# Which up-projection units sum their weights on VectorE: three in the first layer, one in the second

## The chip, the core and the metric

The kernel runs on one core of a Trainium2 chip. Its time is the device time of one launch in microseconds; three runs gave 2179.67, 2180.15 and 2181.21 us (median 2180.15). One more execution was taken with the hardware profiler: it took 2179.59 us, and its span from the first to the last instruction is 2177.8 us. TensorE multiplies, VectorE (DVE) and ScalarE (ACT) do the elementwise work, GpSimd (POOL) and SyncE (SP) issue transfers; POOL also computes a few small powers.

## The reference

Two layers of an encoder on 256 positions of width 2048, all in float32. The part that the change touches is the gated MLP that ends each layer:

```python
D_MODEL, SEQ, D_FF = 2048, 256, 5632

def conv_ffn(x, w_up, conv_w, conv_b, w_down):
    u = x @ w_up                                   # 256 x 11264: gate | value
    up = jnp.pad(u, ((0, 0), (1, 1), (0, 0)))
    c = conv_w.astype(u.dtype)
    u = c[0] * up[:, :-2] + c[1] * up[:, 1:-1] + c[2] * up[:, 2:] + conv_b
    gate, val = jnp.split(u, 2, axis=-1)
    return (jax.nn.silu(gate) * val) @ w_down

for layer in range(2):
    h = rms_norm(x, norm_mix[layer])
    mixed = pool_and_attention(h) if layer == 0 else mlstm_mixer(h)   # shortened
    x = x + mixed
    x = x + conv_ffn(rms_norm(x, norm_ffn[layer]), w_up[layer], ...)
```

## The kernel before

Every product is made of three: an operand is split into a rounded high part and the rest, and high by high, high by low and low by high are summed in PSUM. Weights come from DRAM in chunks of 128 x 1024 (512 KB) through the class `Stream`. `load` issues a chunk's transfer on the SP queue; `split` writes the high part with a copy on ScalarE (L164) and the rest with a subtraction on VectorE (L165) into a tile `hl`. In the MLP, loads run 7 chunks ahead of TensorE and splits 3 chunks ahead, with a few buffers for each.

The order of TensorE's instructions is that of the code. The other engines' orders are made when the kernel is built, except where instructions are pinned (the weight sums on VectorE and the preparing transfers are).

**The MLP of a layer.** The 44 column tiles of the hidden width (128 gate and 128 value columns each) are done in chunks `FCH` of 4, 8, 8, 8, 8, 8 tiles. `up` makes one tile from 4 weight chunks: 64 matmuls, then a sum of two PSUM halves, a multiplication by the row scale, and `tail` (convolution, SiLU, gate, split). `down` multiplies a finished chunk of tiles by the down-projection. `_ffn_plan` lays these out as *slots*, one weight chunk each: a tile is 4 slots, a quarter of a down-projection 2 slots (first chunk) or 4 slots.

**Units.** Some halves of a chunk, four tiles, are done together by `quads` as a 2 x 2 block product with seven block products in place of eight. A unit takes 28 *steps* of 6 matmuls with 512 columns, each from one weight chunk, strewn between the slots: with `(chunk, half, lo, hi, made)` in `UNITS`, step k stands behind slot `lo + k * (hi - lo - 3) / 28` (plus 3 for the last 12 steps). The first 16 steps work through 8 pairs of chunks, the last 12 through 8 chunks with one sum each and 4 without. At its end the four tiles are transposed by `finish` (16 transposes on TensorE) and go through `tail`. A list `late` keeps a unit from starting before the one ahead of it has finished.

The weights of three of the seven products are sums of weight blocks. They are made in one of two ways, by the flag `made`:

- `made` 0: `sums` adds them on VectorE in the chunk just before it is split: per pair one addition in the first chunk (L144) and two in the second (L149, L150), and one more in each of 8 chunks of the last 12 (L147). That is 32 additions of 128 x 512 per unit.
- `made` 1: `make_step` has made them ahead of time in DRAM. Per pair of chunks four parts: twice a copy of half the rows into a DRAM tile `G` on the SP queue (L118) and an accumulating transfer from POOL's queue on top of it (L119), then two accumulating transfers within `G` (L123). The table `make` says beside which weight load each part is issued. The unit then loads `G` instead of the plain weights.

Before, both layers have four units, two of each kind, in turn. Layer 0's 16 prepared pairs are issued during the attention and during layer 0's MLP, layer 1's 16 pairs from 20 chunks before the mLSTM on, 14 chunks apart.

Activation sums for the units (`sums()`, tiles `v` and `sx`) are made once per layer on VectorE and ScalarE at the start of the MLP. `Weave` is the clock that spreads the elementwise pieces: a piece that says `yield 2.5` is issued no sooner than 2.5 us of counted TensorE work later.

Of the kernel before, what the change touches and what calls it, by code (L numbers as in the profile page):

```python
# [237 lines left out]
def trunk(ctx: ExitStack, tc: tile.TileContext, gx, xT, xn, call, catt, cml, weights, make, out):  # L238
# [37 lines left out]
    wv = Weave()  # L276
# [678 lines left out]
    def ffn_layer(layer, norm, nxt):  # L955
        with ExitStack() as es:
# [13 lines left out]
            def tail(u, f, gt, i):  # L970

                y = tp.tile([P, 2, S], F32, tag="y", name=f"y{layer}_{f}")
                for j in range(2):
                    tl = f + j * FT
                    a.activation(y[:, j, :], u[:, j, :], AF.Identity, scale=cw(tl, 1), bias=cw(tl, 3))
                    v.scalar_tensor_tensor(y[:, j, 1:S], u[:, j, 0 : S - 1], cw(tl, 0), y[:, j, 1:S],
                                           ALU.mult, ALU.add)
                    v.scalar_tensor_tensor(y[:, j, 0 : S - 1], u[:, j, 1:S], cw(tl, 2), y[:, j, 0 : S - 1],
                                           ALU.mult, ALU.add)
                s_ = y[:, 0, :]  # L980
                a.activation(s_, s_, AF.Silu)
                v.tensor_mul(s_, s_, y[:, 1, :])
                a.copy(gt[:, i, 0, :], s_)
                v.tensor_sub(gt[:, i, 1, :], s_, gt[:, i, 0, :].bitcast(F32))
# [37 lines left out]
            def product(bank, act, w, c, first, last):  # L1022

                (xh, xl), (wh, wl) = act, (w[:, j, c : c + 512] for j in range(2))
                mm(bank, xh, wh, first, False)
                mm(bank, xh, wl, False, False)
                mm(bank, xl, wh, False, last)
                wv.tick(0.68)

            def block_of(k, t):  # L1030
                return [norm.xx[:, k, j, t * P : t * P + P] for j in range(2)]

            def sum_of(j, p):
                return [sx[:, j, p, i, :] for i in range(2)]

            def quads(fs, c, i0, name):

                def bank(j):
                    return psp.tile([P, 512], F32, tag="ps", name=f"p{j}_{name}")

                def part(j):
                    return cp1.tile([P, 512], F32, tag=f"c{j}", name=f"c{j}_{name}")

                m = KT // 2
                r0, r1 = norm.rcol[:, 0:1], norm.rcol[:, 1:2]
                for p in range(m):
                    ends = p == 0, p == m - 1
                    if p == 0:
                        wv.until(lambda: not late)
                        late.update((0, 2))  # L1050
                    hl = st.next()
                    if p == 0:
                        b1, b5 = bank(1), bank(5)
                    product(b1, block_of(2 * p, 0), hl, 0, *ends)
                    product(b5, sum_of(0, p), hl, 512, *ends)
                    yield
                    hl = st.next()
                    if p == 0:
                        b6, b4 = bank(6), bank(4)
                    product(b6, sum_of(1, p), hl, 0, *ends)  # L1060
                    product(b4, block_of(2 * p + 1, 1), hl, 512, *ends)
                    if p == m - 1:
                        c12, c21, c22 = part(12), part(21), part(22)
                        a.activation(c12, b1, AF.Copy, scale=n0)
                        a.activation(c21, b1, AF.Copy, scale=r1)
                        a.activation(c22, b5, AF.Copy, scale=r1)
                        v.scalar_tensor_tensor(c12, b6, n0, c12, ALU.mult, ALU.add)
                    yield
                for p in range(m):
                    hl = st.next()  # L1070
                    product(b5, sum_of(3, p), hl, 512, False, p == m - 1)
                    product(b6, sum_of(2, p), hl, 0, False, p == m - 1)
                    if p == m - 1:
                        v.scalar_tensor_tensor(c21, b6, r1, c21, ALU.mult, ALU.add)
                        v.tensor_add(c22, c22, c21)
                        v.scalar_tensor_tensor(c21, b4, r1, c21, ALU.mult, ALU.subtract)
                        v.scalar_tensor_tensor(c12, b5, n0, c12, ALU.mult, ALU.add)
                    yield
                    if p % 2:
                        hl = st.next()  # L1080
                        for n in range(2):
                            product(b1, block_of(2 * (p - 1 + n) + 1, 0), hl, n * 512, False, p - 1 + n == m - 1)
                        if p == m - 1:
                            c11 = part(11)
                            a.activation(c11, b1, AF.Copy, scale=r0)
                            gt = g_of(c)
                            wv.add(finish(c12, c22, fs[2:], gt, i0 + 2, name), 3.0)
                            wv.add(finish(c11, c21, fs[:2], gt, i0, name), 5.0)
                        yield

            def finish(top, bottom, fs, gt, i0, name):

                for n, f in enumerate(fs):
                    tr = psp.tile([P, 2, S], F32, tag="ps", name=f"tr{layer}_{f}")
                    for j in range(2):
                        for t, src in enumerate((top, bottom)):
                            c = (2 * j + n) * P
                            pe.transpose(tr[:, j, t * P : t * P + P], src[:, c : c + P], ident)  # L1098
                    u = tp.tile([P, 2, S], F32, tag="tb", name=f"tb_{layer}_{f}")
                    a.copy(u, tr)  # L1100
                    tail(u, f, gt, i0 + n)
                    yield 2.5
                late.discard(i0 % 4)

            def down_end(gt, b, kts):
# [58 lines left out]
            def g_of(c):  # L1164
                if c not in gts:
                    gts[c] = actp.tile([P, 8, 2, S], F32R, tag=f"B{c % 2}", name=f"g{layer}_{c}")
                return gts[c]

            for step in _ffn_plan(layer):
                kind, c = step[:2]  # L1170
                key = step[:3]
                if key not in run:
                    f0 = sum(FCH[:c])
                    run[key] = (up(f0 + step[2], g_of(c), step[2]) if kind == "n" else
                                down(c, gts[c], step[2]) if kind == "d" else
                                quads([f0 + 4 * step[2] + j for j in range(4)], c, 4 * step[2], f"{layer}_{c}{step[2]}"))
                next(run[key], None)
# [64 lines left out]
def _down_chunks(w):  # L1242
# [6 lines left out]


UNITS = (
    ((2, 1, 18, 62, 0), (3, 1, 66, 94, 1), (4, 1, 98, 142, 0), (5, 1, 146, 174, 1)),
    ((2, 1, 18, 62, 0), (3, 1, 66, 94, 1), (4, 1, 98, 142, 0), (5, 1, 146, 174, 1)),
)


# [82 lines left out]
    return out  # L1339


def _make_steps(pairs, places):

    make = {}
    for (key, q), (at, gap) in zip(pairs, places):
        for part in range(4):
            make.setdefault(at + part * gap, []).append((key, part, q))
    return make


def _constants():
# [102 lines left out]
```

## Time and profile before

| | |
|---|---|
| runs, median of 3 | 2180.15 us |
| profiled execution | 2179.59 us |
| its span | 2177.8 us |
| granted TensorE clock | 1.000 |
| first MLP (first `up` to first `mv` matmul of the mLSTM) | 256.0 to 976.6 us |
| mLSTM and its output projection | 976.6 to about 1454.8 us |
| second MLP | about 1454.8 us to the end |
| units of layer 0, first step to last transposition | 310.2-478.2, 486.7-609.1, 614.7-780.0, 788.5-910.8 us |
| units of layer 1 | 1508.9-1678.7, 1687.2-1809.5, 1815.2-1980.0, 1988.5-2110.8 us |

In the rows of the profile, L285 is the line in which nearly all matmuls are recorded, so groups are told apart by their tiles: `up` for tile-wise up-projections, `p` for steps of a unit, `dn` for down-projections, `tr` for a unit's transposes. PE is the row of matmuls, PEld that of weight loads that run beside them. A group's row gives its count, its busy time with the mean of one instruction in ns, and the idle time of its engine just before it with what ended that.

### The profile page before, as it was taken

Reading aid. Unit: us, or ns where it says so; the run is one execution under the profiler, and the core shown is the slowest. Engines: PE = TensorE matmul, PEld = TensorE weight load, DVE = VectorE, ACT = ScalarE, POOL = GpSimd, SP = SyncE. Lnnn points to the kernel's source line nnn. Section 1 sums busy time; section 2 is a strip of 40 time slices with the busy share of each in tenths; the row PEclk is TensorE's granted clock in tenths of the full one; section 3 lists DMA queues with packets and bytes.
Section 4 is the critical chain, followed back from the end, with each engine's and each line's share of the span. In section 5 each row is a group of like instructions: output and inputs, shape, how many; then the busy total and the mean of one; then the engine's idle time right before and its main releaser. Section 6 shows DMA issues by size and latency. Waiting matters only on the chain.

```text
span 2177.8 us, 30504 instructions
## 1 busy us (share of the span) xinstructions
PE 2164.5 (99%) x11040; PEld 1838.1 (84%) x11040; DVE 1711.6 (79%) x2414; ACT 1277.6 (59%) x1808; POOL 133.5 (6%) x168
## 2 busy tenths in 40 slices
PE   9999999999999999999999999999999999999999
PEld 7888888888888888889888888888888888888887
DVE  7686699888798787866767676669888879979785
ACT  7665555666565575655555554556566656556663
POOL 0121101000000000001101010110000000000000
PEclk9999999999999999999999999999999999999999
DMA  8868879889978878769788777877876875767773
GB/s 324 245 217 249 236 234 295 276 264 293 301 235 287 272 232 250 262 202 253 219 248 226 238 229 219 265 223 222 269 244 223 258 247 202 258 232 233 251 232 126
DMA packets 157467, 533.18 MB, mean 245 GB/s; under 512 B 18715, under 2 KB 21059, under 8 KB 156291
## 3 DMA queue, kind: packets, MB, share of 16 engines
q1 hardware_dynamic: 139744, 493.66, 66.2%
q0 software_dynamic: 14496, 33.83, 10.5%
q10 hardware_dynamic: 3074, 3.75, 0.9%
q8 instruction: 86, 1.41, 0.3%
q14 instruction: 67, 0.54, 0.1%
HBM read 529.02 MB, written 69.25 MB: 275 GB/s over the span
## 4 chain that ended last, share of the span: by engine, by line
PE 92%; DVE 6%; issue 1%; ACT 1%; DMA 0%; ACTq 0%; SPq 0%; DVEq 0%
PE up L285 24%; PE dn L285 20%; PE p L285 13%; PE op L285 8%; PE mv L285 4%; PE mq L285 4%; PE mk L285 4%; PE mo L285 4%; PE qproj L285 3%; DVE hl L165 3%; PE pool L285 1%; PE vproj L285 1%; PE kproj L285 1%; ACT hl L164 1%; PE tr L1098 1%
## 5 line engine op out<-in xcount | busy, mean ns | idle before, releaser
L165 DVE TENSOR_TENSOR hl<-w,hl 128x1024 fp32r<-128x1024 f32 (+1 forms) x868 | 1045.0, 1216 | 334.9 <-ACT hl L164 328.1
L164 ACT CAST hl<-w 128x1024 fp32r<-128x1024 f32 (+1 forms) x867 | 897.7, 1048 | 643.7 <-PE up L285 115.8
L285 PE MATMUL up<-xx,hl 128*128 128x512 f32 (+1 forms) x3584 | 647.8, 337 | 0.0
L285 PEld LDWEIGHTS up<-xx,hl 128*128 128x128 f32 x3584 | 563.4, 188 | 87.7 <-DVE hl L165 0.4
L285 PE MATMUL dn<-hl,g 128*128 128x512 f32 x2064 | 492.7, 391 | 0.0
L285 PEld LDWEIGHTS dn<-hl,g 128*128 128x128 f32 x2064 | 385.2, 188 | 78.5
L285 PE MATMUL p<-hl,sx 128*128 128x512 f32 x768 | 206.7, 391 | 3.5 <-DVE hl L165 2.5
L285 PEld LDWEIGHTS p<-hl,sx 128*128 128x128 f32 x768 | 139.4, 188 | 30.6 <-DVE hl L165 3.8
L285 PE MATMUL p<-hl,xx 128*128 128x512 f32 x576 | 157.9, 391 | 4.6 <-DVE hl L165 4.6
L285 PEld LDWEIGHTS p<-hl,xx 128*128 128x128 f32 x576 | 104.5, 188 | 25.3 <-DVE hl L165 6.3
L119 POOL DMA_DIRECT2D G<-in_q x64 | 52.2, 816 | 984.7 <-DMA G<-in_q 972.8
L285 PE MATMUL mk<-xx,hl 128*128 128x512 f32 (+1 forms) x512 | 92.2, 338 | 0.0
L285 PE MATMUL mq<-xx,hl 128*128 128x512 f32 (+1 forms) x512 | 92.2, 338 | 0.0
L285 PE MATMUL mv<-hl,xx 128*128 128x512 f32 (+2 forms) x480 | 91.8, 351 | 0.0
L285 PE MATMUL op<-hl,cat 128*128 128x512 f32 x384 | 91.7, 394 | 0.0
L285 PE MATMUL mo<-hl,xx 128*128 128x512 f32 x384 | 90.6, 392 | 0.0
L285 PE MATMUL op<-hl,mcat 128*128 128x512 f32 x384 | 89.5, 392 | 0.0
L285 PEld LDWEIGHTS mq<-xx,hl 128*128 128x128 f32 x512 | 79.3, 188 | 11.5
L285 PEld LDWEIGHTS mk<-xx,hl 128*128 128x128 f32 x512 | 79.1, 188 | 11.3
L285 PEld LDWEIGHTS mv<-hl,xx 128*128 128x128 f32 x480 | 78.3, 189 | 11.2
L285 PEld LDWEIGHTS op<-hl,mcat 128*128 128x128 f32 x384 | 71.5, 188 | 14.6
L285 PEld LDWEIGHTS mo<-hl,xx 128*128 128x128 f32 x384 | 71.0, 188 | 14.2
(243 smaller groups left out, 1860.8 us busy)
## 6 DMA issues: line engine op xcount, KB each, us to landing
w<-in_up SPq DMA_DIRECT2D x224, 512.0 KB, 4.7
w<-in_dn SPq DMA_DIRECT2D x176, 512.0 KB, 4.6
w<-in_m_in SPq DMA_DIRECT2D x124, 512.0 KB, 5.2
w<-in_q SPq DMA_DIRECT2D x96, 512.0 KB, 4.8
G<-in_q SPq DMA_DIRECT2D x64, 512.0 KB, 5.7
w<-in_a_in SPq DMA_DIRECT2D x46, 512.0 KB, 6.1
G<-in_q POOLq DMA_DIRECT2D x64, 256.0 KB, 6.4
G<-G POOLq DMA_DIRECT2D x64, 256.0 KB, 7.2
```

The costliest lines, as they stand in the source:

```text
L119: pin(add.dma_start(G[r, 0:1024], src[r, 512:1536], accum_op=ALU.add))
L164: (self.nc.vector.tensor_copy if i + c == 0 else self.nc.scalar.copy)(hl[:, 0, c : c + n], w[:, c : c + n])
L165: self.nc.vector.tensor_sub(hl[:, 1, c : c + n], w[:, c : c + n], hl[:, 0, c : c + n].bitcast(F32))
L285: pe.matmul(out_, lhsT, rhs, start=start, stop=stop, skip_group_check=True)
L1098: pe.transpose(tr[:, j, t * P : t * P + P], src[:, c : c + P], ident)
```

## The change

- `UNITS`: layer 0 gets three units, all with sums on VectorE (its unit on chunk 3 is gone, so that those four tiles are done one by one, and the unit on chunk 5 is no longer prepared). They are spread wider: slots 18-74, 81-137 and 144-190, where it was 18-62, 66-94, 98-142, 146-174. Layer 1 keeps four units; the first one is now prepared too, so that three are prepared and one, on chunk 4, sums on VectorE.
- The table of preparing transfers: no pair for layer 0; 24 pairs for layer 1, the first 16 from 20 chunks before the mLSTM on, 13 chunks apart with 6 between the parts, the last 8 in the second MLP, 20 chunks apart with 10 between the parts.
- In `finish`, the four tails of a unit lie farther apart: 4.0 instead of 2.5 us, and the second pair starts 11.0 instead of 5.0 us after the unit's end.

```diff
@@ quads
                             wv.add(finish(c12, c22, fs[2:], gt, i0 + 2, name), 3.0)
-                            wv.add(finish(c11, c21, fs[:2], gt, i0, name), 5.0)
+                            wv.add(finish(c11, c21, fs[:2], gt, i0, name), 11.0)
@@ finish
                     tail(u, f, gt, i0 + n)
-                    yield 2.5
+                    yield 4.0
                 late.discard(i0 % 4)
@@
 UNITS = (
-    ((2, 1, 18, 62, 0), (3, 1, 66, 94, 1), (4, 1, 98, 142, 0), (5, 1, 146, 174, 1)),
-    ((2, 1, 18, 62, 0), (3, 1, 66, 94, 1), (4, 1, 98, 142, 0), (5, 1, 146, 174, 1)),
+    ((2, 1, 18, 74, 0), (4, 1, 81, 137, 0), (5, 1, 144, 190, 0)),
+    ((2, 1, 18, 57, 1), (3, 1, 64, 90, 1), (4, 1, 97, 141, 0), (5, 1, 148, 174, 1)),
 )
@@ kernel
-    make = _make_steps(pairs[0], [(24 + 11 * k, 5) for k in range(8)] + [(len(att) + 30 + 24 * k, 12) for k in range(8)])
-    make.update(_make_steps(pairs[1], [(len(weights) - 20 + 14 * k, 7) for k in range(16)]))
+    places = [[]]
+    at = len(weights) + len(ml)
+    places.append([(at - 182 + 13 * k, 6) for k in range(16)] + [(at + 26 + 20 * k, 10) for k in range(8)])
+    make = {}
+    for l in range(2):
+        _make_steps(make, pairs[l], places[l])
```

The change also moves instructions on VectorE, whose order is made at build time. Two places, both at the first unit of a layer. In the names, the figures behind a tile are its layer, its place and its buffer number; `w` is a raw weight chunk, `hl` its split form, `y` and `tb_up` belong to a tile's tail, `sx` and `v` to the activation sums.

VectorE in layer 0, from the end of the activation sums on, before:

```order
L165 TENSOR_TENSOR hl_3061<-w_2955,hl_3061 128x1024
L976 SCALAR_TENSOR_TENSOR y_3_2919<-tb_up_3_2915,cst,y_3_2919 128x255 x2
L165 TENSOR_TENSOR hl_2984<-w_2868,hl_2984 128x1024
L978 SCALAR_TENSOR_TENSOR y_3_2919<-tb_up_3_2915,cst,y_3_2919 128x255 x2
L165 TENSOR_TENSOR hl_3007<-w_2893,hl_3007 128x1024
L144 TENSOR_TENSOR w_2932<-w_2932 128x512
L450 TENSOR_TENSOR tb_up_4_3044<-up_4_2931,tb_up_4_3044 128x512
L982 TENSOR_TENSOR y_3_2919<-y_3_2919 128x256
L994 TENSOR_TENSOR tb_up_4_3044<-tb_up_4_3044,R_2576 128x512
L165 TENSOR_TENSOR hl_3023<-w_2932,hl_3023 128x1024
```

and after:

```order
L976 SCALAR_TENSOR_TENSOR y_3_2868<-tb_up_3_2864,cst,y_3_2868 128x255 x2
L978 SCALAR_TENSOR_TENSOR y_3_2868<-tb_up_3_2864,cst,y_3_2868 128x255 x2
L165 TENSOR_TENSOR hl_2932<-w_2820,hl_2932 128x1024
L165 TENSOR_TENSOR hl_2953<-w_2842,hl_2953 128x1024
L165 TENSOR_TENSOR hl_2968<-w_2881,hl_2968 128x1024
L144 TENSOR_TENSOR w_2904<-w_2904 128x512
L450 TENSOR_TENSOR tb_up_4_2990<-up_4_2880,tb_up_4_2990 128x512
L165 TENSOR_TENSOR hl_3021<-w_2930,hl_3021 128x1024
L982 TENSOR_TENSOR y_3_2868<-y_3_2868 128x256
L165 TENSOR_TENSOR hl_3044<-w_2951,hl_3044 128x1024
```

All rows ahead of these are the same in both. `hl_2984` and `hl_2932` are the same chunk, the second one of the unit; before, another chunk's split stands ahead of it. The third chunk of the unit, which is added to and split here before (`w_2932`, `hl_3023`), now stands behind the splits of two plain chunks, since its step comes one slot later.

VectorE in layer 1, at the same place, before:

```order
L150 TENSOR_TENSOR w_13363<-w_13363 128x512
L1019 TENSOR_TENSOR sx_12945<-v_13136,sx_12945 128x4x128
L976 SCALAR_TENSOR_TENSOR y_3_13414<-tb_up_3_13410,cst,y_3_13414 128x255 x2
L978 SCALAR_TENSOR_TENSOR y_3_13414<-tb_up_3_13410,cst,y_3_13414 128x255 x2
L165 TENSOR_TENSOR hl_13478<-w_13363,hl_13478 128x1024
L165 TENSOR_TENSOR hl_13499<-w_13388,hl_13499 128x1024
L144 TENSOR_TENSOR w_13427<-w_13427 128x512
L450 TENSOR_TENSOR tb_up_4_13536<-up_4_13426,tb_up_4_13536 128x512
L165 TENSOR_TENSOR hl_13571<-w_13476,hl_13571 128x1024
L982 TENSOR_TENSOR y_3_13414<-y_3_13414 128x256
L149 TENSOR_TENSOR w_13497<-w_13497,w_13427 128x512
```

and after:

```order
L1019 TENSOR_TENSOR sx_12843<-v_13035,sx_12843 128x4x128
L165 TENSOR_TENSOR hl_13415<-w_13325,hl_13415 128x1024
L165 TENSOR_TENSOR hl_13454<-w_13349,hl_13454 128x1024
L976 SCALAR_TENSOR_TENSOR y_3_13312<-tb_up_3_13308,cst,y_3_13312 128x255 x2
L450 TENSOR_TENSOR tb_up_4_13436<-up_4_13324,tb_up_4_13436 128x512
L165 TENSOR_TENSOR hl_13468<-w_13373,hl_13468 128x1024
L978 SCALAR_TENSOR_TENSOR y_3_13312<-tb_up_3_13308,cst,y_3_13312 128x255 x2
L165 TENSOR_TENSOR hl_13491<-w_13395,hl_13491 128x1024
```

The additions (L144, L149, L150) are gone from between the splits, and two splits now follow the last row of the activation sums at once.

More of the change, by code (lines that the diff above doesn't have):

```diff
@@ L1339, in _with_prep, with _make_steps @@
     return out
-def _make_steps(pairs, places):
-    make = {}
+def _make_steps(make, pairs, places):
     for (key, q), (at, gap) in zip(pairs, places):
@@ L1347, in _make_steps @@
             make.setdefault(at + part * gap, []).append((key, part, q))
-    return make
 def _constants():
```

## The prediction

> **What bounds the kernel now.** I read the page's busy shares first, then TensorE's waits, then the chain of waits for the price of single pieces, then busy time by stretches. Busy shares:
>
> ```profile
> PE 2164.5 (99%) x11040; PEld 1838.1 (84%) x11040; DVE 1711.6 (79%) x2414; ACT 1277.6 (59%) x1808; POOL 133.5 (6%) x168
> ```
>
> Matmuls fill 99% of the span of 2177.8 us. What TensorE lost to others is in the list of waits, first its weight loads', then its matmuls' own:
>
> ```profile
> PEld p L285 <- DVE hl L165: 10.1, 10, 2.0
> PEld p L285 <- ACT hl L164: 1.4, 2, 0.9
> ...
> PE p L285 <- DVE hl L165: 7.1, 8, 1.7
> PE p L285 <- ACT hl L164: 1.0, 2, 0.7
> ```
>
> The columns are us in total, times, longest. Both show the same twelve or so events: steps of units (`p`) that wait for a weight chunk's split. The load rows (11.5 us) count too much, since a load waits while a matmul still runs; the matmul rows (8.1 us) count too little, since matmul spans overlap. I take 10 us as the loss. No row of TensorE waits for a transfer. So the kernel is bound by the number of matmuls, with 10 us of stalls on top; a change can win at most these and must pay for every added matmul.
>
> Where they lie, by the load waits in the windows 256-480, 610-790, 1455-1680 and 1812-1985 us:
>
> ```profile
> PEld p L285 <- DVE hl L165: 2.7, 4, 1.1
> PEld p L285 <- ACT hl L164: 0.5, 1, 0.5
> ...
> PEld p L285 <- DVE hl L165: 1.7, 1, 1.7
> ...
> PEld p L285 <- DVE hl L165: 4.5, 4, 2.0
> PEld p L285 <- ACT hl L164: 0.9, 1, 0.9
> ...
> PEld p L285 <- DVE hl L165: 1.2, 1, 1.2
> ```
>
> These are the four units that sum on VectorE: 3.2 and 1.7 us in layer 0, 5.4 and 1.2 us in layer 1. The four prepared units lose nothing. Busy time in five stretches says why (PE, PEld, DVE, ACT, POOL, clock, DMA share, GB/s):
>
> ```profile
> 311.00:346.00 35.00, 33.03 (x164) 26.93 (x163) 32.90 (x48) 20.63 (x28) 3.23 (x4) 1.00 0.82 254
> 480.00:610.00 130.00, 130.00 (x645) 109.95 (x644) 103.04 (x131) 82.40 (x106) 8.15 (x10) 1.00 0.88 281
> 610.00:636.00 26.00, 24.67 (x120) 20.45 (x119) 25.96 (x44) 16.80 (x26) 1.61 (x2) 1.00 0.84 256
> 1509.00:1594.00 85.00, 80.98 (x416) 68.18 (x416) 77.80 (x106) 51.15 (x67) 4.04 (x5) 1.00 0.78 250
> 1680.00:1812.00 132.00, 132.00 (x657) 111.70 (x656) 105.04 (x134) 82.84 (x107) 0.00 (x0) 1.00 0.73 237
> ```
>
> Where TensorE lost time VectorE was busy 92 to 100%; in a prepared unit (second and last row) it is at 79 to 80% and TensorE runs through, with DMA shares of 0.88 and 0.73 alike.
>
> **Lost unit: four more tiles one by one.** Prices from the chain of waits (start, us, what), and the group of the tiles' weight loads:
>
> ```profile
> 362.16 1.37 PE p L285 x6
> 394.01 11.14 PE up L285 x64
> 603.38 0.44 PE tr L1098 x4
> 659.06 5.44 PE dn L285 x24
> ...
> L285 PEld LDWEIGHTS up<-xx,hl 128*128 128x128 f32 x3584 | 563.4, 188 | 87.7 <-DVE hl L165 0.4
> ```
>
> Four tiles: 4 x 11.14 = 44.56 us. A unit: 28 steps x 1.37 + 4 x 0.44 for its 16 transposes = 40.12 us. TensorE is full, so all of the difference is on the path: +4.4 us. The same tiles come out, so down-projections don't change, nor does the weight kind that is read last; whether a unit is summed or prepared, it has the same matmuls.
>
> A rule speaks against this price. The Trainium skill (Perfetto Trace Analysis, Identifying the Most-Contended Engine) says that matmul busy time is a bad measure of TensorE and weight-load busy share a good one. By it the loads would be the price: at the row's 188 ns, four tiles' 256 loads against a unit's 168 (transposes left out) would cost 88 x 0.188 = 16.5 us in place of 4.4, and the sum below would end 12 us higher. The trace disagrees: 64 loads of 188 ns are 12.0 us, and the tile took 11.14.
>
> **VectorE's load at the units.** Groups that make it up:
>
> ```profile
> L165 DVE TENSOR_TENSOR hl<-w,hl 128x1024 fp32r<-128x1024 f32 (+1 forms) x868 | 1045.0, 1216 | 334.9 <-ACT hl L164 328.1 <-DMA w<-in_q 1.6
> ...
> L459 DVE TENSOR_TENSOR x<-x,dn 128x512 f32<-128x512 f32 x94 | 60.5, 681 | 11.5 <-PE dn L285 11.5
> L978 DVE SCALAR_TENSOR_TENSOR y<-tb_up,cst,y 128x255 f32<-128x255 f32 x112 | 51.0, 475 | 0.0
> L976 DVE SCALAR_TENSOR_TENSOR y<-tb_up,cst,y 128x255 f32<-128x255 f32 x112 | 49.0, 476 | 0.2
> L450 DVE TENSOR_TENSOR tb_up<-up,tb_up 128x512 f32<-128x512 f32 x56 | 38.5, 687 | 26.1 <-ACT tb_up L449 25.8
> L994 DVE TENSOR_TENSOR tb_up<-tb_up,R 128x512 f32<-128x512 f32 x56 | 38.4, 686 | 0.9
> L984 DVE TENSOR_TENSOR g<-y,g 128x256 fp32r<-128x256 f32 x88 | 36.6, 416 | 0.0
> L982 DVE TENSOR_TENSOR y<-y 128x256 f32<-128x256 f32 x88 | 36.6, 416 | 0.6 <-ACT y L981 0.6
> L144 DVE TENSOR_TENSOR w<-w 128x512 f32<-128x512 f32 x32 | 21.8, 682 | 0.0
> ```
>
> By busy time over count: a split 1.20 us, a weight sum 0.68; a tile beside its splits (38.5 + 38.4 + 51.0 + 49.0) / 56 + 2 x 36.6 / 88 = 3.99, so 1.00 a slot. An `up` slot thus costs VectorE 2.20 us for 11.14 / 4 = 2.79 of TensorE. A `dn` slot costs 1.20 plus two additions of 0.64 in 4 slots, 1.53, or in 2 slots, 1.85 (first chunk), for 2.72. A step of a summed unit's first part costs 1.20 + 1.5 x 0.68 = 2.23 for 1.37, of a prepared one 1.20. Between two steps stand (hi - lo - 3) / 28 slots. That gives VectorE's work over TensorE's:
>
> - layer 0, first unit, before: 1.46 slots, four fifths `up`, 5.35 / 5.43 = 0.98. After: 1.89 slots, 6.27 / 6.62 = 0.95.
> - the summed unit on chunk 4, before, both layers: 1.46 slots, half `up`, 4.96 / 5.40 = 0.92. After in layer 1: the same 0.92. After in layer 0: 1.89 slots, two thirds `up`, 5.97 / 6.60 = 0.90.
> - the unit on chunk 5 in layer 0, prepared before, now summed: 1.54 slots, 5.10 / 5.59 = 0.91.
> - layer 1, first unit, before 0.98; after, prepared: 1.29 slots, 3.94 / 4.93 = 0.80.
>
> **What becomes of the stalls.** At 0.98 a unit lost 3.2 and 5.4 us (mean 4.3), at 0.92 1.7 and 1.2 (mean 1.45), at 0.80 and less nothing. On that line the three units of layer 0 lose 1.45 + 0.03 / 0.06 x 2.85 = 2.9, then 1.2 and 1.3; I round to 2.6, 1.2 and 1.2, since the tails of the unit ahead, which ran into the start of the second summed unit (25.96 busy in 26 us above), are spread out. Layer 1 loses 0 and 1.2. Sum 6.2 in load waits against 11.5, in real loss 10 x 6.2 / 11.5 = 5.4: -4.6 us. Bounds: at least about 1.4 us stays, the first wait of layer 0's first unit (the 0.5 us on ScalarE above and, by the load waits from 311 to 318 us, 1.1 on VectorE: 1.6, or 1.4 real), for whose chunk the same additions are queued as before:
>
> ```profile
> PEld p L285 <- DVE hl L165: 1.1, 1, 1.1
> ```
>
> At most each unit of layer 0 loses what its first one does now, 3.2, and layer 1's last one 1.2: 10.8 in load waits, 9.4 real. So -8.6 to -0.6 us.
>
> **Preparing transfers.** 32 pairs become 24:
>
> ```profile
> L123 POOL DMA_DIRECT2D G<-G x64 | 59.1, 923 | 177.7 <-DMA G<-in_q 132.7 <-DMA G<-G 38.7 <-issue 6.2
> ...
> L119 POOL DMA_DIRECT2D G<-in_q x64 | 52.2, 816 | 984.7 <-DMA G<-in_q 972.8 <-issue 11.9
> ...
> G<-in_q SPq DMA_DIRECT2D x64, 512.0 KB, 5.7
> ...
> G<-G POOLq DMA_DIRECT2D x64, 256.0 KB, 7.2
> ```
>
> Each pair is two SP issues and four POOL issues; the eight that go save POOL 2 x (0.82 + 0.92) = 3.5 us each, worth nothing: nobody on the path waits for POOL, which idled 985 us before its rows for the copies to land. SP loses 16 issues in layer 0, where weight transfers were never awaited: nothing. In the second MLP eight pairs are new, one in 20 chunks; layer 0's MLP held one in 24 at a share of 0.88 and TensorE ran through, so nothing again, 0 to 1 us as a bound (the longest wait of a step is 2.0 us now, and one late pair would be about that). The last part of the last pair is issued at chunk 196 of the second MLP; its unit starts at slot 148 plus 84 steps, chunk 232: 36 chunks of about 2.4 us between them, against a landing of 7.2. POOL's powers stand behind accumulations that wait for their copy; that held before in the mLSTM and lost TensorE nothing.
>
> **Tails apart.** The last tail comes 15 us after a unit, before 7.5. Nothing is added. A unit ends at the latest 8 slots (some 20 us) ahead of the next; the last of layer 1 at slot 173 of 184, its tiles read from 184 on, 30 us later. Cost 0, bounds -0.5 to +1 us.
>
> **Sum.** 2179.6 (profiled execution) + 4.4 - 4.6 + 0 = 2179.4. The median of the runs lies 0.56 above that execution, so 2179.9. Unknowns: 4.4 - 8.6 - 0.5 = -4.7 and 4.4 - 0.6 + 2 = +5.8 from 2180.15: 2175.4 to 2186; with the load waits' 11.5 us as the loss the lower end would be 1.4 lower, so I give 2175 to 2186.
>
> **Rivals.** Within 0.2% (4.36 us) is about what a measurement here can't tell from no change.
>
> 1. Stalls go, faster: the spread does its work and only the first wait stays, 2180.15 + 4.4 - 8.6 = 2176.0, and 2174.6 if the loss is really the load waits' 11.5 us. It speaks for it that all units of the new plan are below 0.98; against it that both units at 0.92 still lost over a microsecond. Chance 0.18, about 0.12 of it past the edge of 2175.8.
> 2. VectorE becomes the bound of layer 0, slower: three summed units in one layer hold 3 x 32 x 0.68 = 65 us of additions, before 44. If backlog carries over from unit to unit, each loses what layer 1's first one did, 5.4: 3 x 5.4 + 1.2 = 17.4 load waits, 15.1 real, 2180.15 + 4.4 + 5.1 = 2189.7. It turns to slower when the stalls reach 10 us again, 3.0 us real a unit in layer 0. Against it, the ratios of 0.90 to 0.95. Chance 0.10.
> 3. Prepared blocks late in layer 1: one late landing of 7.2 us before a unit's step shows as a wait of a load `w<-G`; two of them and TensorE loses 14, minus 4.6 plus 4.4: 2194. Against it, the 36 chunks. Chance 0.02.
> 4. Weight loads set TensorE's pace: four tiles cost 16.5 us more, 2192. Against it, the tile's 11.14 us under the sum of its loads. The rule of the Trainium skill weighed above gives this. Chance 0.01.
> 5. The change does nothing on the path but lose the unit (stalls as before, 10 us): 2184.6, just at the edge. Chance 0.06, half of it beyond the edge.
>
> That leaves 0.63 for the forecast, all within 0.2%. Faster 0.12, slower 0.10 + 0.02 + 0.01 + 0.03 = 0.16, same 0.63 + 0.06 + 0.03 = 0.72. The range 2175 to 2186 takes in most of rival 1, rival 5 and the near part of 2.
>
> **What would show it.** The profile after should have 60 x 64 = 3840 `up` matmuls and 7 x 168 = 1176 of `p`; no wait of `p` around the first unit of layer 1; waits of `p` at three places in layer 0, the first near 314 us, none over 3 us; VectorE under 95% in them; no wait on `w<-G`. Wrong would be the forecast if a stretch of layer 0 shows VectorE full and TensorE losing over 3 us a unit, if TensorE's loads wait for a transfer, or if tiles cost more than 11.14 us.

## The result: faster by 0.28%

The changed kernel takes 2174.27 us (median of 8 runs, 2174.08 to 2174.59), the kernel before in the same session 2180.49 us (8 runs, 2179.67 to 2181.28). The ratio is 0.9972, with a 95% interval of 0.9961 to 0.9982: 6.2 us less. The forecast was 2179.9, 0.2 us under the 2180.15 of the kernel before, and no measurable change. The result lies under the forecast range. The profiled executions differ by 5.3 us (2179.59 and 2174.26; spans 2177.8 and 2172.5).

The busy shares on the page of the kernel after:

```profile
PE 2166.4 (100%) x11112; PEld 1845.1 (85%) x11112; DVE 1704.5 (78%) x2405; ACT 1268.8 (58%) x1792; POOL 107.3 (5%) x136
```

TensorE has 72 matmuls more than before, and is busy 1.9 us longer in a span 5.3 us shorter. So it was not work that went, but waiting. The waits of TensorE's loads and matmuls for splits (us in total, times, longest):

```profile
PEld p L285 <- DVE hl L165: 1.7, 2, 1.5
...
PE p L285 <- DVE hl L165: 1.2, 1, 1.2
```

Before, these rows stood at 10.1 and 7.1 us, and ScalarE's splits added 1.4 and 1.0; those rows are gone. By windows all of the 1.7 us lie in the first unit of layer 0 (256 to 480 us), and the loads have no wait for a split anywhere behind it. The groups have the numbers of the plan:

```profile
L285 PE MATMUL up<-xx,hl 128*128 128x512 f32 (+1 forms) x3840 | 693.7, 337 | 0.0
L285 PEld LDWEIGHTS up<-xx,hl 128*128 128x128 f32 x3840 | 604.3, 188 | 93.8
...
L285 PE MATMUL p<-hl,sx 128*128 128x512 f32 x672 | 179.5, 390 | 0.0
...
L285 PE MATMUL p<-hl,xx 128*128 128x512 f32 x504 | 137.1, 390 | 1.2 <-DVE hl L165 1.2
```

Busy time in the three units of layer 0, and in the first and third unit of layer 1 (columns as in the prediction):

```profile
310.30:519.10 208.80, 207.61 (x1077) 176.84 (x1075) 180.58 (x245) 125.24 (x164) 0.00 (x0) 1.00 0.69 225
526.10:733.10 207.00, 207.00 (x1064) 176.35 (x1063) 174.89 (x232) 122.86 (x159) 0.00 (x0) 1.00 0.70 226
740.10:918.40 178.30, 178.30 (x895) 151.17 (x893) 151.59 (x198) 104.00 (x131) 1.67 (x2) 1.00 0.74 242
1510.20:1670.50 160.30, 160.30 (x839) 137.02 (x838) 131.63 (x176) 102.52 (x135) 11.46 (x15) 1.00 0.92 284
1808.40:1981.10 172.70, 172.70 (x861) 146.21 (x861) 148.15 (x194) 101.25 (x128) 4.03 (x5) 1.00 0.78 249
```

Four of the five run through at a VectorE share of 82 to 86%. The forecast had put 1.2 us of waits into each of the second, third and fifth row.

The ratios of the prediction are for the first part of a unit. About that part of layer 0's first unit and of layer 1's unit on chunk 4, before:

```profile
310.00:404.00 94.00, 92.03 (x477) 77.51 (x476) 84.68 (x114) 55.50 (x73) 6.49 (x8) 1.00 0.85 273
...
1815.00:1909.00 94.00, 93.15 (x460) 78.63 (x459) 84.02 (x113) 55.33 (x73) 0.00 (x0) 1.00 0.70 238
```

and after:

```profile
310.30:430.00 119.70, 118.51 (x628) 101.33 (x627) 107.81 (x148) 72.19 (x96) 0.00 (x0) 1.00 0.69 227
...
1808.40:1907.00 98.60, 98.60 (x489) 83.46 (x489) 86.65 (x112) 56.82 (x71) 4.03 (x5) 1.00 0.81 261
```

VectorE is busy 90% of the first before and after, and 89 and 88% of the second, while TensorE loses 2.0 and 1.2 us, and 0.9 and nothing. So VectorE's load hardly changed where the losses did.

Two stretches are enough to follow the time through all the runs: layer 0's MLP (its first `up` to the first `mv`) and layer 1's MLP (its first `up` to the end). Between them lie 478.05 to 478.06 us in every kernel, and ahead of them 256 us, but for one run. From the starts in each trace, in us (the kernels with splits pinned in order are left out):

| kernel | span | layer 0's MLP | layer 1's MLP | stalls of TensorE over 0.25 us in the two |
|---|---|---|---|---|
| before | 2177.8 | 720.7 | 723.1 | 4.2 + 5.8 |
| after | 2172.5 | 721.8 | 716.6 | 1.4 + 0 |
| wider tails alone | 2180.6 | 723.0 | 723.6 | 5.3 + 5.7 |
| after, old tails | 2172.1 | 721.7 | 716.4 | 1.4 + 0 |
| layer 0's part alone | 2173.9 | 721.7 | 718.1 | 1.4 + 1.5 |
| layer 1's part alone | 2174.2 | 720.7 | 719.4 | 4.2 + 2.3 |
| after, first unit narrow | 2174.6 | 723.8 | 716.6 | 2.7 + 0 |
| after, layer 0 as layer 1 | 2174.2 | 715.8 | 720.4 | 0 + 3.1 |
| before, other extra buffers | 2173.1 | 720.7 | 718.5 | 4.2 + 1.5 |
| after, other extra buffers | 2176.0 | 721.9 | 720.0 | 1.4 + 2.9 |
| four units, extra buffers placed | 2166.5 | 715.6 | 716.8 | 0 + 0 |

A stall here is what the distance between the starts of two matmuls exceeds its usual value by; small ones are left out, so a stretch can grow by somewhat more. The change costs layer 0 1.2 us (721.84 against 720.66) and gives layer 1 6.6 us (716.58 against 723.15).

### The profile page after: what moved, and what is told of

It reads as the page before. It is cut to its first block, busy times and chain, and to the rows that moved or that the text cites. A ratio compares the mean times of both kernels' runs of the same rounds, so it can differ in the third digit from the quotient of the medians.

```text
span 2172.5 us, 30459 instructions
## 1 busy us (share of the span) xinstructions
PE 2166.4 (100%) x11112; PEld 1845.1 (85%) x11112; DVE 1704.5 (78%) x2405; ACT 1268.8 (58%) x1792; POOL 107.3 (5%) x136
## 4 chain that ended last, share of the span: by engine, by line
PE 98%; DVE 1%; issue 0%; ACT 0%; DVEq 0%
PE up L285 29%; PE dn L285 22%; PE p L285 12%; PE op L285 8%; PE mv L285 4%; PE mq L285 4%; PE mk L285 4%; PE mo L285 4%; PE qproj L285 3%; PE pool L285 1%; PE kproj L285 1%; PE vproj L285 1%; PE tr L1098 1%; PE av L285 1%; PE qk L285 1%; DVE hl L165 1%
## 5 line engine op out<-in xcount | busy, mean ns | idle before, releaser
L165 DVE TENSOR_TENSOR hl<-w,hl 128x1024 fp32r<-128x1024 f32 (+1 forms) x856 | 1032.8, 1217 | 326.1 <-ACT hl L164 317.8
L164 ACT CAST hl<-w 128x1024 fp32r<-128x1024 f32 (+1 forms) x855 | 887.7, 1048 | 654.2 <-PE up L285 150.6
L285 PE MATMUL up<-xx,hl 128*128 128x512 f32 (+1 forms) x3840 | 693.7, 337 | 0.0
L285 PEld LDWEIGHTS up<-xx,hl 128*128 128x128 f32 x3840 | 604.3, 188 | 93.8
L285 PE MATMUL p<-hl,sx 128*128 128x512 f32 x672 | 179.5, 390 | 0.0
L285 PEld LDWEIGHTS p<-hl,sx 128*128 128x128 f32 x672 | 121.3, 188 | 21.9 <-DVE hl L165 0.2
L285 PE MATMUL p<-hl,xx 128*128 128x512 f32 x504 | 137.1, 390 | 1.2 <-DVE hl L165 1.2
L285 PEld LDWEIGHTS p<-hl,xx 128*128 128x128 f32 x504 | 91.3, 188 | 18.1 <-DVE hl L165 1.5
L119 POOL DMA_DIRECT2D G<-in_q x48 | 38.8, 808 | 1233.5 <-DMA G<-in_q 1202.5
L285 PEld LDWEIGHTS mq<-xx,hl 128*128 128x128 f32 x512 | 79.4, 188 | 11.5
```

The lines of the kernel that those rows point to most:

```text
L119: pin(add.dma_start(G[r, 0:1024], src[r, 512:1536], accum_op=ALU.add))
L164: (self.nc.vector.tensor_copy if i + c == 0 else self.nc.scalar.copy)(hl[:, 0, c : c + n], w[:, c : c + n])
L165: self.nc.vector.tensor_sub(hl[:, 1, c : c + n], w[:, c : c + n], hl[:, 0, c : c + n].bitcast(F32))
L285: pe.matmul(out_, lhsT, rhs, start=start, stop=stop, skip_group_check=True)
```

## The experiments

Two theories were held against each other. By the *load theory*, the prediction's, a unit loses time as VectorE's work per step nears TensorE's. By the *order theory*, a step waits because the build's order has put its chunk's split behind splits of later chunks; I call such a chunk *overtaken*, by as many chunks as went ahead of it.

### The tails alone, and the change without them

```diff
@@ wider tails alone: before with
-                            wv.add(finish(c11, c21, fs[:2], gt, i0, name), 5.0)
+                            wv.add(finish(c11, c21, fs[:2], gt, i0, name), 11.0)
-                    yield 2.5
+                    yield 4.0
@@ after, old tails: after with
-                            wv.add(finish(c11, c21, fs[:2], gt, i0, name), 11.0)
+                            wv.add(finish(c11, c21, fs[:2], gt, i0, name), 5.0)
-                    yield 4.0
+                    yield 2.5
```

> The kernel before with the wider tails alone (units and transfers as before). If VectorE's load per step makes the stalls, they stay: first units 3.2 and 5.4 us of load waits, the units on chunk 4 1.7 and 1.2, time within 0.5 us of the kernel before. If the pile-up of tails makes those at chunk 4, these 2.9 us go: about 2.9 us faster, and the first units keep theirs.

> The changed kernel with the old tails. Load theory: nothing comes back, 2174.3 us within 0.5. Tail theory: the summed units that start behind another one (chunk 4 and 5 in layer 0, chunk 4 in layer 1) lose 1 to 1.7 us each again, 2177 to 2179 us.

Measured: the wider tails alone give 2183.18 us against 2181.27, ratio 1.0011 (1.0001 to 1.0021), so if anything a little slower. The load wait from 610 to 790 us, 1.7 us before, did not go but grew:

```profile
PEld p L285 <- DVE hl L165: 2.5, 1, 2.5
```

The change with the old tails gives 2174.03 us, 0.9967 (0.9954 to 0.9980), the same as with the new. The tails have no part in the gain.

### Each layer's part alone

```diff
@@ layer 0's part alone: before with
-    ((2, 1, 18, 62, 0), (3, 1, 66, 94, 1), (4, 1, 98, 142, 0), (5, 1, 146, 174, 1)),
+    ((2, 1, 18, 74, 0), (4, 1, 81, 137, 0), (5, 1, 144, 190, 0)),
@@ and no transfers for layer 0's pairs
@@ layer 1's part alone: before with
-    ((2, 1, 18, 62, 0), (3, 1, 66, 94, 1), (4, 1, 98, 142, 0), (5, 1, 146, 174, 1)),
+    ((2, 1, 18, 57, 1), (3, 1, 64, 90, 1), (4, 1, 97, 141, 0), (5, 1, 148, 174, 1)),
@@ and the new places of layer 1's 24 pairs
```

> Layer 0's three units alone, layer 1 and the tails as before. The lost unit costs 4.4 to 4.9 us. Load theory: layer 0's stalls fall from 4.9 to about 1.4 us, layer 1 keeps 6.6: 1 to 1.5 us slower than before. Tail theory: the second and third unit lose 1 to 1.7 us each, 3 to 4.5 us slower than before.

> Layer 1's units and prepared pairs alone, layer 0 and the tails as before. The first unit's 5.4 us go in any case: about 5 us faster than before, 2175 us. Load theory: the unit on chunk 4, whose step spacing is unchanged, keeps about 1.2 us. Tail theory: the same, since the tails are the old ones. If it loses nothing, its new place, further from the unit ahead, did it.

Measured: 2175.72 us, 0.9975 (0.9965 to 0.9985), and 2175.97 us, 0.9978 (0.9969 to 0.9988). Each half gives most of the whole gain: 5.5 and 5.3 us against 6.2 together. So they don't add up, and both runs hold something that neither half's text says.

With layer 0's part alone the code of layer 1's units is that of before, and yet layer 1's MLP fell from 723.1 to 718.1 us. Its load waits from 1455 to 1680 us, 4.5 and 0.9 before:

```profile
PEld p L285 <- DVE hl L165: 1.8, 2, 1.1
```

With layer 1's part alone its first unit loses nothing, but its unit on chunk 4 does, which loses nothing in the kernel after with the same units, pairs and slots. From 1812 to 1985 us:

```profile
PEld p L285 <- DVE hl L165: 2.0, 3, 1.1
PEld p L285 <- ACT hl L164: 1.2, 1, 1.2
```

What differs in both cases is the number of a chunk in layer 1. A unit reads 28 chunks and the four tiles that it replaces 16; with three units in layer 0 all later chunks are numbered 12 lower. In `Stream.home` the number has an effect: a chunk with `i % 5 == 4` has its split written into an extra buffer, and one with `i % 7 == 6` is loaded into one. This gave the order theory.

### Layer 0 like layer 1

```diff
@@ after with
-    ((2, 1, 18, 74, 0), (4, 1, 81, 137, 0), (5, 1, 144, 190, 0)),
+    ((2, 1, 18, 57, 1), (3, 1, 64, 90, 1), (4, 1, 97, 141, 0), (5, 1, 148, 174, 1)),
-    places = [[]]
+    places = [[(10 + 8 * k, 4) for k in range(8)] + [(78 + 10 * k, 5) for k in range(8)] + [(162 + 16 * k, 8) for k in range(8)]]
```

> The changed kernel with layer 0's units and preparing transfers like layer 1's: four units, three of them prepared, one summing on chunk 4. The fourth unit gives back 4.4 to 4.9 us of matmuls, and the first one, prepared, its wait of 1.4. Order theory (a stall comes where the build's order puts another chunk's split ahead of two or more earlier ones): layer 0's unit on chunk 4 has no such place and loses nothing, layer 1's has four and loses 1.5 to 2.5 us: 2169.5 to 2171 us. Load theory: both lose about 1.4 us, 2170.5 to 2171.5. If 24 prepared pairs in layer 0 come too late, its loads of prepared blocks wait and it is slower than 2174.

Measured: 2176.25 us, 0.9979 (0.9969 to 0.9988). Layer 0's MLP lost nothing at all and took 715.8 us. Two losses took the gain away. Layer 1, whose chunks are numbered as before again, lost 3.1 us in its unit on chunk 4. And the attention lost about 4 us: the first `up` starts at 260.0 in place of 256.0 us. Its wait on TensorE's loads, and VectorE just ahead of it (start, us, what, idle before):

```profile
PEld tr_k L542 <- DVE rot_k L533: 2.5, 2, 2.1
```

```profile
53.26 0.43 DVE L507 TENSOR_TENSOR qt_q<-qproj,tab 128x256 f32<-128x256 f32 x1 [2.78 <-ACT hsq_q L498]
53.60 1.28 DVE L533 TENSOR_TENSOR rot_k<-rot_k,re_qk 128x512 f32<-128x512 f32 x2
```

`re_qk`, which `rot_k` needs, was done at 50.5 us; VectorE stood idle for 2.78 us in front of a row that waited for ScalarE, and `rot_k` was queued behind it. This too is an order made at build time. That the early pairs caused it wasn't tested by itself; the last run below, with later pairs, has `rot_k` at 50.3 us.

### All splits pinned in program order

To take the overtaking away altogether, the splits of the MLPs were pinned in the order of the code on ScalarE and VectorE: in the kernel before, in the kernel after, and in the one with layer 0 like layer 1.

```diff
@@ split
-            (self.nc.vector.tensor_copy if i + c == 0 else self.nc.scalar.copy)(...)
-            self.nc.vector.tensor_sub(...)
+            pin = self.tc.keep_in_program_order if self.more else (lambda e: e)
+            pin((self.nc.vector.tensor_copy if i + c == 0 else self.nc.scalar.copy)(...))
+            pin(self.nc.vector.tensor_sub(...))
```

> The kernel before, units, transfers and tails untouched, with the splits of the MLPs kept in the order of their chunks on ScalarE and VectorE. Load theory: the four summed units still lose about 10 us, within 1 us of the kernel before. Order theory: the waits fall to 2 us or less, 2171 to 2173 us.

> The changed kernel with the splits of the MLPs kept in the order of their chunks. Order theory: the one wait left (1.4 us at 321 us) goes, 2172.5 to 2174 us. Load theory: no change, 2174.3. A strict order could also hold up splits behind a late chunk: then over 2175.

> Four units in both layers, three of each prepared, splits kept in order. Order theory: no stalls to speak of, 2174.3 - 4.9 - 1.4 = 2168 us. Load theory: about 2.9 us of waits at the two summed units, 2171 us.

Measured: 2389.94 us (1.0960, 1.0942 to 1.0978), 2356.83 us (1.0803, 1.0786 to 1.0820) and 2349.26 us (1.0768, 1.0752 to 1.0784). The longest waits of the first:

```profile
PEld dn L286 <- ACT hl L165: 53.1, 26, 3.3
PEld p L286 <- DVE hl L166: 30.6, 29, 2.6
PEld dn L286 <- DVE hl L166: 28.8, 26, 1.4
```

The pin holds the splits in their order among all the other pinned pieces too, and now down-projections wait, which never did. In the first kernel TensorE's loads wait 175.8 us for splits in the MLPs, and the granted clock is 0.972 in place of 1.000. Losses of 173 to 209 us hide an effect of a few, so these runs decide nothing between the theories. They show only that this pin costs far more than the few misses of the free order.

### Other chunks in the extra buffers

One line moves the extra buffers to other chunks and nothing else: no unit, slot, pair, tail or instruction count changes, so no engine gets more or less work. In the kernel before, layer 1 gets the numbering that it has with three units in layer 0; in the kernel after, it gets that of four. (The added line shifts the line numbers by one: the splits are L165 and L166, the matmuls L286.)

```diff
@@ home, in before
+        i += -12 if i > 500 else 0
         return ((self.wpool if i % 7 < 6 else self.more[0]) if raw else
                 (self.spool if i % 5 < 4 else self.more[1]))
@@ home, in after
+        i += 12 if i > 500 else 0
```

> The kernel before; in layer 1 alone the rule that gives every fifth chunk a buffer of its own counts from another chunk, so that the same work is done in the same steps with other chunks in the extra buffer. With it no chunk of layer 1's four units has its split behind the splits of two or more later chunks, as three had in the kernel before. Order theory: TensorE's stalls in layer 1's four units fall from about 5.8 us to about 1.5 us, as where only layer 0 was changed, layer 0 keeps its stalls at 314, 320, 343 and 634 us, and the time is 2180.3 - 4.3 = about 2176. Load theory (the loss follows the ratio of VectorE's load to TensorE's in a step, which this edit doesn't touch): no change, 2180.3.

> The kernel after; in layer 1 alone the rule of the extra buffer counts from another chunk, as it did where layer 1 alone was changed. Three or four chunks of the unit with the fourth chunk of rows then have their splits behind those of two or three later ones. Order theory: that unit loses 2.3 to 3.0 us in three or four waits, as it did there, and the time is about 2174.3 + 2.5 = 2177. Load theory: no change, 2174.3.

Measured: 2175.64 us, 0.9975 (0.9965 to 0.9986), for the first; 2177.49 us, 0.9983 (0.9974 to 0.9993), for the second. So the kernel before gained 5.8 us from this line, nearly all that the whole change gains, and the kernel after, at 2174.27 in its own session, lost 3.2 us by it. The load waits of the first in the four windows of the prediction (256-480, 610-790, 1455-1680 us, and none from 1812 to 1985):

```profile
PEld p L286 <- DVE hl L166: 2.7, 4, 1.1
PEld p L286 <- ACT hl L165: 0.5, 1, 0.5
...
PEld p L286 <- DVE hl L166: 1.8, 1, 1.8
...
PEld p L286 <- DVE hl L166: 1.8, 2, 1.1
```

Layer 0 is as before; layer 1 lost 5.4 and 1.2 us before and loses 1.8 now. Its first unit in the kernel before and in this one, over the same stretch:

```profile
1508.90:1678.70 169.80, 165.78 (x858) 140.41 (x858) 150.00 (x203) 101.43 (x133) 4.04 (x5) 1.00 0.74 244
```

```profile
1508.90:1678.70 169.80, 168.65 (x878) 143.42 (x877) 153.53 (x209) 104.53 (x137) 4.05 (x5) 1.00 0.77 248
```

VectorE is busier, at 90% in place of 88%, and TensorE loses 1.2 us in place of 4.0. A ratio of loads can't do that. Nor did weights come earlier: in layer 1's MLP no split of the kernel before waits for a transfer, and in the moved one such waits are 0.3 us in all. What the line changes is the order. VectorE at the place of before's longest stall (1517 us, 1.9 us):

```profile
1515.54 1.20 DVE L165 TENSOR_TENSOR hl<-w,hl 128x1024 fp32r<-128x1024 f32 x1
1516.67 0.41 DVE L982 TENSOR_TENSOR y<-y 128x256 f32<-128x256 f32 x1
1517.01 0.67 DVE L149 TENSOR_TENSOR w<-w,w 128x512 f32<-128x512 f32 x1
1517.61 0.67 DVE L994 TENSOR_TENSOR tb_up<-tb_up,R 128x512 f32<-128x512 f32 x1
1518.21 2.34 DVE L165 TENSOR_TENSOR hl<-w,hl 128x1024 fp32r<-128x1024 f32 x2
```

and in the moved kernel:

```profile
1515.50 2.36 DVE L166 TENSOR_TENSOR hl<-w,hl 128x1024 fp32r<-128x1024 f32 x2
1517.77 0.69 DVE L995 TENSOR_TENSOR tb_up<-tb_up,R 128x512 f32<-128x512 f32 x1
1518.37 1.23 DVE L166 TENSOR_TENSOR hl<-w,hl 128x1024 fp32r<-128x1024 f32 x1
```

The rows have no chunk numbers. With them, from the order made at build time:

```
before: split 575, split 576, sum in 577, tail, split 579, tail, sum in 580, tail, split 577, split 578
moved:  split 575, tail, split 577, split 578, tail, split 579, sum in 580, tail, split 581
```

TensorE wants 577, 578, 579. In the kernel before, 579 has the extra buffer (579 % 5 is 4) and its split, with three other pieces, went ahead of the split of 577. Moved, 579 waits its turn, and the stall is gone.

The second kernel's waits from 1812 to 1985 us, where the kernel after has none:

```profile
PEld p L286 <- DVE hl L166: 2.6, 3, 1.1
PEld p L286 <- ACT hl L165: 1.2, 1, 1.2
```

Which of the two extra buffers does it, the loaded or the split chunk's, was not separated by a run: the line moves both. The orders of all the kernels point to the split chunk's. In each of the 43 stalls that the end of a split ends (counted below) a chunk of the extra split buffer is either the one that went ahead (30) or the one overtaken (13); a chunk of the extra buffer for loads is among them in 22.

### The first unit of layer 0 narrow again

```diff
@@ after with
-    ((2, 1, 18, 74, 0), (4, 1, 81, 137, 0), (5, 1, 144, 190, 0)),
+    ((2, 1, 18, 62, 0), (4, 1, 81, 137, 0), (5, 1, 144, 190, 0)),
```

> The kernel after with the first unit of layer 0 spread over 44 weight chunks instead of 56, as before, so that its splits fall due as densely as they did; all else as after. Load theory: the ratio of that unit goes back from 0.95 to 0.98, and the stalls that the kernel before had there (2.7 us from 314 to 343) return in place of 1.4: about 2175.6. Order theory: the same two chunks as before are overtaken by two or three later ones, so the stalls of 314 and 320 return, about 2.1 us in place of 1.4: 2175.0 to 2175.6.

Measured: 2176.25 us, 0.9976 (0.9966 to 0.9986), 2.0 us over the kernel after. From 256 to 480 us:

```profile
PEld p L285 <- DVE hl L165: 2.8, 4, 1.1
PEld p L285 <- ACT hl L164: 0.5, 1, 0.5
```

These are before's stalls of 314, 320 and 343 us in place of the one of 321. So the spread of the first unit is worth 2 us; the edit moves both the load per step and the order, so this run doesn't say by which. Here the order theory, as I had put it, missed: the splits that end the three stalls belong to chunks overtaken by one only, where I had counted on two or three, and it had not foreseen that of 343 us. And both theories put the time at least 0.6 us too low.

### Four units, with the extra buffers placed

The kernel with layer 0 like layer 1, with its first pairs begun later and layer 1's extra buffers moved, so that in the units no chunk is overtaken by more than one.

```diff
@@ layer 0 like layer 1, with
-    places = [[(10 + 8 * k, 4) for k in range(8)] + [(78 + 10 * k, 5) for k in range(8)] + [(162 + 16 * k, 8) for k in range(8)]]
+    places = [[(24 + 7 * k, 3) for k in range(8)] + [(80 + 10 * k, 5) for k in range(8)] + [(162 + 16 * k, 8) for k in range(8)]]
@@ home
+        i += -12 if i > 500 else 0
```

> The kernel after with layer 0's MLP in layer 1's four units, of which three are prepared by accumulating transfers, the transfers of its first unit begun later than in the run with layer 0 as layer 1 (whose attention lost about 4 us), and the extra buffers of layer 1 counted so that no chunk is behind two or more others. Order theory: it saves the fourth unit's price, 4.9 us, and the one stall of 1.4 us that the kernel after still has in layer 0, and loses nothing in layer 1: 2174.3 - 6.3 = about 2168. If the transfers still hold up the attention's start, some 4 us come on top, about 2172. Load theory: layer 1's unit of the fourth chunk, which was at a ratio of 0.92, loses its 2 to 3 us as it did in that run, 2171.

Measured: 2168.27 us (2168.24 to 2168.40), 0.9940 (0.9926 to 0.9955). It beats both kernels: 13 us under the 2181.43 of the kernel before in the same session, and 6.0 us under the kernel after, which was measured in another session (2174.27). Its chain of waits by engine, and the only waits that its loads have:

```profile
PE 100%; DVE 0%; issue 0%
```

```profile
PEld wps L310 <- DVE pad L679: 1.2, 1, 1.2
PEld kproj L286 <- DVE hl L166: 0.6, 2, 0.4
PEld kproj L286 <- DVE xx L352: 0.2, 1, 0.2
```

All of these are at the program's start or in the attention; no step of a unit waits. Layer 1's unit on chunk 4, for which the load theory asked 2 to 3 us again, loses nothing.

### What all the traces say together

Taken over eleven kernels (all but the three pinned ones), VectorE writes 6804 chunk splits for the two MLPs; 353 of them, 5%, are overtaken by the order made at build time. TensorE's stalls over 0.25 us in the MLPs are 54. Of these 43 end when the split of an overtaken chunk ends: 30 of these chunks are overtaken by one, 13 by two or three. The other 11 stand beside such a stall in the same step, 10 directly ahead of it, which end with ScalarE's half of the same split, and one directly behind it. No other split ever ended one.

But most overtaken chunks cost nothing: 303 of the 333 that are overtaken by one, and 7 of the 20 overtaken by two or three. The last kernel has 19 and no stall. The expectations counted on two or more, and counted too many of these: in the kernel before one chunk of layer 1 (609) is overtaken by more than one, not three. What the moved buffers took away there is that 577, 587 and 609 are overtaken at all. Where a chunk overtaken by a single one cost something (30 stalls), it was, but for two, in the first unit of a layer with sums on VectorE. I read from this that the order says which step can wait, and the load how much is felt of it. The first half is shown by the moved buffers for layer 1; in layer 0 it rests on the stalls counted here, since no run moves its order alone. The second half is not shown: no run changes the load at an unchanged order.

## Why the prediction was wrong, step by step

- **The bound was right.** In the kernels before and after the time is the number of matmuls plus the stalls. The Trainium skill (Perfetto Trace Analysis, Identifying the Most-Contended Engine), as the prediction weighed it, takes the weight loads' busy share for a good measure of TensorE. Priced by the loads the lost unit would have cost 16.5 us; in the runs it was 4.9, with the loads' share at 85% and the chain of the last kernel at 100% matmuls.
- **The step that failed is "What becomes of the stalls".** It drew a line through the units' losses over their load ratio and read 2.6, 1.2 and 1.2 us for layer 0 and 1.2 for layer 1 from it, 5.4 us real. Left were 1.4 us in all: the units at ratios of 0.90, 0.91 and 0.92 lost nothing. The same unit at the same ratio lost 0 or 2.9 us as one line moved the extra buffers (after, and after with other extra buffers), and layer 1's first unit 4.0 or 1.2 at the same work. VectorE's measured share in the units hardly changed (90 and 90%, 89 and 88%). So the load ratio did not set the losses; the order of splits set where they came. It stands in the quoted rows on the change: before, the split of the unit's second chunk (`hl_2984`) follows that of a later one (`hl_3061`). The prediction gave that shift no cost.
- **Unforeseen: layer 0's edit changed layer 1.** With 12 chunks less in layer 0, layer 1's extra buffers fall on other chunks. The kernel before gained 5.8 us when only they were moved, and the kernel after lost 3.2 when they were moved back. No step of the prediction had it. It and the prepared first unit each take away that unit's stalls, so their gains don't add.
- **The loss before was put too low.** I took 10 us between the matmuls' 8.1 and the loads' 11.5. Layer 1's MLP with no stall is 6.6 us shorter (723.15 against 716.58), layer 0's with four units and no stall 5.1 us (720.66 against 715.59): 11.6 us. The loads' rows were right within 0.1 us.
- **The lost unit was put too low.** Layer 0 takes 721.8 us with three units, 1.4 of it a stall, and 715.6 with four and no stall: 4.9 us in place of 4.4. Which of the two prices, the tiles' or the unit's, is off is not shown.
- **The sum, with measured terms:** -11.6 + 1.4 + 4.9 = -5.3, and the profiled spans differ by 5.3. It is the table's rows added up, so it shows the size of the terms and is no test of them. The forecast had -10 + 5.4 + 4.4 = -0.2: of its miss of 5.1, 4.0 lie in the stalls that were to stay, 1.6 in the loss before, and 0.5 the other way in the lost unit.
- **The least stall was 1.4 us by luck.** The prediction's lower bound kept 1.4 us for the first wait of layer 0, at 314 us. That wait is gone (0.2 us from 311 to 318). The stall of 1.4 us is one at 321.5 us for the unit's third chunk, which is overtaken by two: in the quoted rows after, the splits of two plain chunks (`hl_3021`, `hl_3044`) stand ahead of it. The lower end of the range failed all the same. The prediction worked out 2175.4 with a loss of 10 us, and 1.4 less, 2174.0, with the loads' 11.5 us, which the runs bear out; it gave 2175.
- **Right: the prepared first unit of layer 1** lost nothing, the transfers cost nothing (no load waits for `G`), and the tails cost and gave nothing. That the wider tails would relieve the second summed unit, for which I rounded its loss down, is not borne out: with them alone its wait was 2.5 us in place of 1.7. Layer 0 loses 32 copies on the SP queue, two for each of 16 pairs, where the prediction says 16; they cost nothing either way.
- **Rival 1 came nearest:** it gave 2176.0, and 2174.6 with the loads' 11.5 us as the loss. Measured 2174.27. But "only the first wait stays" is not what happened, and the spread that was to do the work is worth 2 us by the run with the first unit narrow; the number is in part luck. I held it at 0.18 since both units at 0.92 had lost something; with the order as cause that was no evidence against it. Rivals 2 to 5 did not come: VectorE was at 82 to 86% in the units, no block was late, tiles did not cost 16.5 us more, and the stalls did not stay.

## What to carry to other kernels

Where an order is made at build time and buffers are uneven (an extra one for every fifth chunk), a stall is a matter of which piece stands behind which: look up the piece that ended each wait in the order before fitting losses to loads. An edit early in a program can move the stalls far behind it by shifting the numbering on which buffers rest; so an effect can show in code that was not touched, and a measured gain is not yet the merit of what the edit meant to do. When a loss is to be sized from waits of loads and of matmuls, compare a stretch that has the stalls with one that has not.

## What was not expected of the hardware

Nothing in the runs asked for a new behaviour of the chip. One bound went further than the trace of before had shown: transfers were taken as harmless up to a share of 0.88, and in the last kernel, which prepares sums for both layers, TensorE ran through the first unit of layer 0 (160.30 us busy of 160.30) at a share that the profile gives as 1.01, and 322 GB/s:

```profile
310.30:470.60 160.30, 160.30 (x839) 136.94 (x838) 131.72 (x176) 102.77 (x135) 21.04 (x27) 1.00 1.01 322
```
